# A transformer encoder in two fp32r halves: the weights' halves start at a different place in each chunk's buffers

## The chip, the cores and the metric

One core of a Trainium2 chip runs the kernel. The time is device microseconds from start to end of one execution; for a kernel on one core that is this core's time. Runs of a kernel are compared on the same chip. TensorE multiplies, VectorE and ScalarE do the element-wise work, GpSimd (POOL) helps, and SyncE (SP) issues the weights' loads.

## The reference

A two-layer encoder on one sequence of 256 tokens with 1024 channels, all in float32:

```
for l in range(2):
    h = rms_norm(x, g_mix[l])
    c_q, c_kv, k_r, qkv_b, qkv_c, gate_logits = split(h @ w_in[l])
    y_a = latent attention (8 heads)           # w_uq, w_ukv
    y_b = dilated banded attention (12 heads)
    y_c = neighbourhood attention with a bias (8 heads)
    gates = sigmoid(gate_logits)               # three of 1024
    merged = gates[0]*(y_a @ w_pa[l]) + gates[1]*(y_b @ w_pb[l]) + gates[2]*(y_c @ w_pc[l])
    x = x + merged @ w_o[l]
    h = rms_norm(x, g_ffn[l])
    x = x + (silu(h @ w1[l]) * (h @ w3[l])) @ w2[l]    # 2816 inner channels
return rms_norm(x, g_final)
```

## The kernel before

Every large product is made of fp32r pieces: an operand is cast to fp32r (its high half, hi), the rest is subtracted out (its low half, lo), and three products, hi x hi, hi x lo and lo x hi, are summed in PSUM. XH and XL are the halves of the normed input (8 blocks of 128 channels by 256 tokens), YH and YL those of the attention outputs, HL those of the merged and of the gated inner channels, chl those of the latent vectors.

The weights (158 MB with both layers) are packed on the host into 308 chunks, 154 for each layer, mostly 128 partitions by 1024 columns, in the order in which they are used (`plan`). Each chunk passes through three steps. `dma_next` loads it into one of 6 buffers `raw`, on SP's queue. `split_next` casts it to `hi` on ScalarE (line 292) and subtracts on VectorE to get `lo` (line 294), into one of 4 buffers each. `take` hands the pair to the products, and before that keeps the loads 6 chunks and the split 1 chunk ahead of the use.

`mm3` (line 320) makes the three products for one block of 128 x 128 weights and 256 tokens, all through line 318, where TensorE first loads the weights and then streams the other operand through. `n_tile` runs it for the 8 blocks of a chunk: 24 products into one half of a PSUM bank. The blocks of a chunk lie 512 bytes apart in each partition, the blocks of XH and XL 1024. In some parts the roles are exchanged: activations are loaded as weights, and hi or lo is streamed (values of the attentions, 256 or 288 columns; the last w2 products, 512 columns).

Each layer goes through projections and attentions (other small products between, from queues of units), the gate logits (24 chunks), the merge of the three branches with `w_o`, the first two inner blocks in 4 merged chunks `f`, and then 20 steps of w1, w3 and w2 chunks: the feed-forward. The order on each engine is that of a planner that simulates the program; a few instructions are tied to others by hand (`queue`).

Tiles are laid in SBUF one after another in a pool, each size rounded up to 32 bytes: first the pool `one` (X, XH, XL, C, G, YH, YL, RB, RT), then `ring` (raw, hi, lo), then `tmp` with everything else. `single` and the `tile_pool` lines show the sizes.

Of the kernel before, what the change touches and what calls it, by code (L numbers as in the profile page):

```python
# [11 lines left out]
F32R = mybir.dt.float32r  # L12
# [4 lines left out]
P = 128  # L17
# [210 lines left out]
def f32(ap):  # L228
    return ap.bitcast(F32)
# [3 lines left out]
def encoder(ctx: ExitStack, tc: tile.TileContext, x, w, gains, cst, rpb, gfin, out):  # L233
# [4 lines left out]
    ring = ctx.enter_context(tc.tile_pool(name="ring", bufs=4))  # L238
# [23 lines left out]
    def queue(ins, behind):  # L262
        info = mybir.DependencyInfo(mybir.DependencyClass.NoSync, mybir.DependencyReason.DATA)
        tc.add_manual_dep(ins, behind.name, info, reason="order")
# [21 lines left out]
    def split_next():  # L286
        i = at["split"]
        width = chunks[i][2]
        t = raw.pop(i)
        hi = ring.tile([P, 1024], F32R, tag="hi", name="hi", bufs=4)  # L290
        lo = ring.tile([P, 1024], F32R, tag="lo", name="lo", bufs=4)
        act.copy(hi[:, :width], t[:, :width])  # L292
        eng = pool if chunks[i][1] == ("f", 0) else dve
        ins = eng.tensor_sub(lo[:, :width], t[:, :width], f32(hi[:, :width])).ins  # L294
        if eng is dve and "hold" in at:
            queue(ins, at["hold"])
        split[i] = (hi, lo)
        at["split"] += 1

    def ahead(n_split, n_dma):  # L300
        n = len(chunks)
        while at["split"] < min(n, n_split):
            while at["dma"] <= at["split"]:
                dma_next()
            split_next()
        while at["dma"] < min(n, n_dma):
            dma_next()
# [813 lines left out]
```

## Time and profile before

| | |
|---|---|
| time, median of 3 runs | 926.07 us (923.6 to 926.31) |
| profiled execution: time, span | 925.92 us, 924.1 us |
| busy share of PE, PEld, DVE, ACT, POOL | 98%, 94%, 72%, 56%, 14% |
| granted TensorE clock, mean | 0.997 |
| bytes read from HBM | 157.64 MB, 172 GB/s over the span |

PE is TensorE's products, PEld its weight loads, which run beside products. A product's duration in the profile is from its start to the end of the last column's result, some 0.28 us, and products overlap; how fast they follow each other is seen from their start times in the timeline. A line of the chain of waits that says "5.60 PE ps_g L318 x48" means that for 5.60 us the end was set by 48 products in a row. Distances in bytes are counted in one partition, from the tile sizes in the code.

### The profile page before, as it was taken

Reading aid. Unit: us, or ns where it says so; the run is one execution under the profiler, and the core shown is the slowest. Engines: PE = TensorE matmul, PEld = TensorE weight load, DVE = VectorE, ACT = ScalarE, POOL = GpSimd, SP = SyncE. Lnnn points to the kernel's source line nnn. Section 1 sums busy time; section 2 is a strip of 40 time slices with the busy share of each in tenths; the row PEclk is TensorE's granted clock in tenths of the full one; section 3 lists DMA queues with packets and bytes.
Section 4 is the critical chain, followed back from the end, with each engine's and each line's share of the span. In section 5 each row is a group of like instructions: output and inputs, shape, how many; then the busy total and the mean of one; then the engine's idle time right before and its main releaser. Section 6 shows DMA issues by size and latency. Waiting matters only on the chain. (4 is left out here: it accounts for less than half of the span.)

```text
span 924.1 us, 18598 instructions
## 1 busy us (share of the span) xinstructions
PE 906.0 (98%) x7446; PEld 871.0 (94%) x7446; DVE 660.8 (72%) x1003; ACT 519.1 (56%) x858; POOL 128.9 (14%) x138
## 2 busy tenths in 40 slices
PE   8999999999999999999999999999999999999996
PEld 6999898999999999999999989899999999999995
DVE  6987877555888766666699888665577976666663
ACT  6776875533566544444477778655355654444443
POOL 2223112000022100000023240400000210000000
PEclk9999999999999999999999999999999999999998
DMA  8985455344675766655467644533457566555531
GB/s 290 286 289 174 133 149 150 107 153 148 193 223 183 258 209 195 184 185 184 119 237 213 211 147 135 173 117 124 145 178 214 168 212 205 184 193 184 195 124 45
DMA packets 53414, 166.71 MB, mean 180 GB/s; under 512 B 6736, under 2 KB 7504, under 8 KB 53328
## 3 DMA queue, kind: packets, MB, share of 16 engines
q1 hardware_dynamic: 48384, 158.69, 53.7%
q0 software_dynamic: 1920, 3.15, 1.6%
q10 hardware_dynamic: 3024, 3.69, 1.5%
q8 instruction: 58, 0.95, 0.4%
q14 instruction: 28, 0.23, 0.1%
HBM read 157.64 MB, written 1.05 MB: 172 GB/s over the span
## 5 line engine op out<-in xcount | busy, mean ns | idle before, releaser
L294 DVE TENSOR_TENSOR lo<-raw,hi 128x1024 fp32r<-128x1024 f32 (+4 forms) x306 | 373.3, 1227 | 153.4 <-ACT hi L292 152.1
L292 ACT CAST hi<-raw 128x1024 fp32r<-128x1024 f32 (+5 forms) x308 | 304.1, 992 | 301.8 <-PE ps_g L318 162.7
L318 PE MATMUL ps_g<-XH,hi 128*128 128x256 f32 x1392 | 390.0, 281 | 1.2 <-ACT hi L292 1.2
L318 PE MATMUL ps_g<-XH,lo 128*128 128x256 f32 x1392 | 387.9, 281 | 1.6 <-DVE lo L294 1.6
L318 PE MATMUL ps_g<-XL,hi 128*128 128x256 f32 x1392 | 389.3, 280 | 0.0
L318 PEld LDWEIGHTS ps_g<-XH,hi 128*128 128x128 f32 x1392 | 261.5, 188 | 5.2 <-issue 1.9
L318 PEld LDWEIGHTS ps_g<-XH,lo 128*128 128x128 f32 x1392 | 260.2, 188 | 5.3 <-issue 2.7
L318 PEld LDWEIGHTS ps_g<-XL,hi 128*128 128x128 f32 x1392 | 261.7, 188 | 1.6 <-issue 0.3
L318 PE MATMUL ps_acc<-HL,hi 128*128 128x256 f32 x608 | 109.3, 279 | 0.0
L318 PEld LDWEIGHTS ps_acc<-HL,hi 128*128 128x128 f32 x608 | 93.1, 188 | 0.0
L318 PE MATMUL ps_acc<-HL,lo 128*128 128x256 f32 x304 | 84.2, 280 | 0.0
L995 POOL TENSOR_TENSOR SG<-fab 128x256 f32<-128x256 f32 x44 | 34.5, 786 | 305.7 <-DVE fab L991 302.5
L318 PEld LDWEIGHTS ps_acc<-HL,lo 128*128 128x128 f32 x304 | 57.1, 188 | 0.0
L318 PE MATMUL ps_acc<-hi,HL 128*128 128x512 f32 x176 | 55.3, 395 | 0.0
L318 PE MATMUL ps_g<-hi,XL 128*128 128x256 f32 (+1 forms) x160 | 45.9, 287 | 0.0
L318 PE MATMUL ps_g<-hi,XH 128*128 128x256 f32 (+1 forms) x160 | 45.4, 284 | 0.0
L318 PE MATMUL ps_g<-lo,XH 128*128 128x256 f32 (+1 forms) x160 | 45.2, 285 | 0.0
L991 DVE TENSOR_TENSOR fab<-ps_g,RB 128x512 f32<-128x512 f32 x40 | 27.6, 691 | 21.9 <-PE ps_g L318 21.9
L528 ACT COPY pT<-ps_t 128x512 f32<-128x512 f32 (+1 forms) x48 | 26.0, 551 | 29.0 <-PE ps_t L518 21.8
L318 PEld LDWEIGHTS ps_acc<-hi,HL 128*128 128x128 f32 x176 | 31.7, 188 | 6.1
L318 PE MATMUL ps_acc<-lo,HL 128*128 128x512 f32 x88 | 34.8, 395 | 0.0
L834 POOL TENSOR_TENSOR t<-t,CSR 128x512 f32<-128x512 f32 x12 | 19.7, 1644 | 107.9 <-DMA t<-t 79.1
(194 smaller groups left out, 1263.0 us busy)
## 6 DMA issues: line engine op xcount, KB each, us to landing
raw<-in_w SPq DMA_DIRECT2D x250, 512.0 KB, 3.6
raw<-in_w SPq DMA_DIRECT2D x20, 384.0 KB, 3.1
raw<-in_w SPq DMA_DIRECT2D x16, 320.0 KB, 3.1
braw<-in_rpb SPq DMA_DIRECT2D x16, 256.0 KB, 5.2
raw<-in_w SPq DMA_DIRECT2D x16, 256.0 KB, 2.7
t<-t ACTq DMA_DIRECT2D x48, 64.0 KB, 4.4
raw<-in_w SPq DMA_DIRECT2D x4, 432.0 KB, 4.9
KCt<-KCt POOLq DMA_DIRECT2D x8, 128.0 KB, 5.8
```

Source lines behind the costliest of these rows:

```text
L292: act.copy(hi[:, :width], t[:, :width])
L294: ins = eng.tensor_sub(lo[:, :width], t[:, :width], f32(hi[:, :width])).ins
L318: pe.matmul(o, a, b, start=start, stop=stop, skip_group_check=True)
L528: act.copy(u.pT[:, :n], u.tr[:, :n])
L834: pool.tensor_mul(t13, t13, bc(SR, 2))
L991: dve.tensor_mul(ab, o.rearrange("p (n s) -> p n s", n=2), bc(RB, 2))
L995: pool.tensor_mul(s[:, 1, :], ab[:, 0, :], ab[:, 1, :])
```

## The change

In the n-th chunk (n counts over both layers) hi and lo no longer begin at the start of their buffers, but 4 (n mod 14) columns, 16 (n mod 14) bytes, after it. The buffers get 52 columns more, which is the largest such shift. What is loaded, cast, subtracted and multiplied is the same, in the same order; the tiles that are laid after these buffers move up by the added bytes.

```diff
--- before.py
+++ after.py
@@ -287,8 +287,10 @@
         i = at["split"]
         width = chunks[i][2]
         t = raw.pop(i)
-        hi = ring.tile([P, 1024], F32R, tag="hi", name="hi", bufs=4)
-        lo = ring.tile([P, 1024], F32R, tag="lo", name="lo", bufs=4)
+
+        skew = slice(4 * (i % 14), 4 * (i % 14) + 1024)
+        hi = ring.tile([P, 1024 + 52], F32R, tag="hi", name="hi", bufs=4)[:, skew]
+        lo = ring.tile([P, 1024 + 52], F32R, tag="lo", name="lo", bufs=4)[:, skew]
         act.copy(hi[:, :width], t[:, :width])
         eng = pool if chunks[i][1] == ("f", 0) else dve
         ins = eng.tensor_sub(lo[:, :width], t[:, :width], f32(hi[:, :width])).ins
```

## Rows read from the trace of the kernel before

**Rows 1.** Page, part 1: busy us (share of the span) and instructions of each engine.
```profile
PE 906.0 (98%) x7446; PEld 871.0 (94%) x7446; DVE 660.8 (72%) x1003; ACT 519.1 (56%) x858; POOL 128.9 (14%) x138
```

**Rows 2.** Waits of TensorE: line, releaser, us in total, times, longest us.
```profile
PE ps_s L318 <- POOL KB L836: 2.6, 2, 1.5
...
PE ps_g L318 <- DVE lo L294: 1.6, 3, 0.6
...
PE ps_g L318 <- ACT hi L292: 1.2, 1, 1.2
```

**Rows 3.** Chain of waits in order of time: start us, us, products.
```profile
706.28 2.83 PE ps_acc L318 x24
...
764.57 5.60 PE ps_g L318 x48
770.17 2.79 PE ps_acc L318 x12
```

**Rows 4.** Windows: us, each engine's busy us and operations, granted clock, DMA.
```profile
186.00:226.00 40.00, 40.00 (x341) 40.00 (x341) 20.76 (x24) 13.49 (x15) 0.00 (x0) 1.00 0.47 145
...
304.00:454.00 150.00, 150.00 (x1284) 150.00 (x1283) 97.85 (x109) 68.00 (x91) 14.16 (x18) 1.00 0.63 196
...
760.00:900.00 140.00, 140.00 (x1001) 130.98 (x1000) 91.69 (x102) 63.09 (x84) 12.60 (x17) 1.00 0.56 181
```

**Rows 5.** Timeline: transposes in the feed-forward of layer 1.
```profile
743.02 1.47 PE L1003 MATMUL ps_acc<-C,X 128*128 128x128 f32 x12
```

**Rows 6.** Groups: line, engine, tiles, shapes, count, busy us, mean ns, idle before.
```profile
L294 DVE TENSOR_TENSOR lo<-raw,hi 128x1024 fp32r<-128x1024 f32 (+4 forms) x306 | 373.3, 1227 | 153.4 <-ACT hi L292 152.1
L292 ACT CAST hi<-raw 128x1024 fp32r<-128x1024 f32 (+5 forms) x308 | 304.1, 992 | 301.8 <-PE ps_g L318 162.7
L318 PE MATMUL ps_g<-XH,hi 128*128 128x256 f32 x1392 | 390.0, 281 | 1.2 <-ACT hi L292 1.2
...
L318 PE MATMUL ps_acc<-HL,hi 128*128 128x256 f32 x608 | 109.3, 279 | 0.0
...
L318 PE MATMUL ps_acc<-hi,HL 128*128 128x512 f32 x176 | 55.3, 395 | 0.0
L318 PE MATMUL ps_g<-hi,XL 128*128 128x256 f32 (+1 forms) x160 | 45.9, 287 | 0.0
...
L318 PE MATMUL ps_g<-YL,hi 128*128 128x256 f32 x96 | 27.0, 281 | 0.0
...
L318 PE MATMUL ps_c<-YH,hi 128*128 128x256 f32 x64 | 18.0, 282 | 0.0
```

**Rows 7.** Timeline: ends of the first w1 tile, layer 0, then layer 1.
```profile
287.66 0.28 PE L318 MATMUL ps_g<-XH,hi 128*128 128x256 f32 x1
...
290.37 0.28 PE L318 MATMUL ps_g<-XH,lo 128*128 128x256 f32 x1
...
740.73 0.28 PE L318 MATMUL ps_g<-XH,lo 128*128 128x256 f32 x1
...
742.48 0.28 PE L318 MATMUL ps_g<-XH,lo 128*128 128x256 f32 x1
```

**Rows 8.** Timeline: the first merged chunk f, layer 0.
```profile
276.19 0.28 PE L318 MATMUL ps_f<-XH,hi 128*128 128x256 f32 x1
...
279.07 0.28 PE L318 MATMUL ps_f<-XH,hi 128*128 128x256 f32 x1
```

**Rows 9.** Timeline: products of the latent tile, layer 0.
```profile
46.78 0.39 PE L318 MATMUL ps_a<-chl,hi 128*128 128x256 f32 x2
...
47.46 0.39 PE L318 MATMUL ps_a<-chl,hi 128*128 128x256 f32 x2
```

**Rows 10.** Timeline: products of the attention outputs in the merge.
```profile
225.53 0.28 PE L318 MATMUL ps_g<-YH,hi 128*128 128x256 f32 x1
...
228.37 0.28 PE L318 MATMUL ps_g<-YH,hi 128*128 128x256 f32 x1
```

## Prediction

> **What bounds the kernel now.** I read the page's first part first: TensorE's products are busy for 906.0 of 924.1 us and its weight loads for 871.0, while VectorE stands at 72% [rows 1]. The table of waits, cut to TensorE, comes next: six groups of waits, 9.5 us in all, the longest 2.6 us [rows 2]. So no load, cast or subtraction is late. The end is set by how fast TensorE starts one product after another, and the change can move it in only two ways: by that rhythm, or by making the two halves late.
>
> The page's list of costly groups shows 281 ns for a product, but that is a latency; neighbours overlap. The rhythm is read from start times. In the first tile of the feed-forward 23 steps take from 287.66 to 290.37, 117.8 ns each [rows 7]; later in that stretch the chain has pieces of 48 products in 5.60 us, 116.7 ns each [rows 3]. Over long windows: 40 us hold 341 products and 150 us hold 1,284. As the products in flight at both edges are counted, I add one latency of 0.28 us and get 118.1 and 117.0 ns. [...] A stream of transposes, which move 128 columns instead of 256 behind weights of the same size, starts every 109 ns (12 in 1.47 us, less one latency, over 11) [rows 5]. So about 8 ns of each product is something other than its weight load, and this is what the change could reach.
>
> **Part 1: the rhythm.** Products that read hi or lo, counted from the groups (the third product of a trio has half the count where two share hi): 3 x 1392 and 3 x 160 into ps_g, 608 + 304 into ps_acc, 3 x 96 into ps_g and 3 x 64 into ps_c from YH and YL, as many as the latter into ps_f, together 6,240 of about 256 columns, and 176 + 88 = 264 of 512 columns [rows 6]. So 1 ns of rhythm is worth 6.2 us.
>
> Where operands lie follows from the tile sizes, each rounded up to 32 bytes: hi and lo start 224 bytes (modulo 512) past XH and XL, 448 past HL and the latent tile chl, 32 past YH. All slices step by multiples of 512, so these distances now hold for every product of a kind. After the change a buffer has 4,304 bytes, laid out as 4,320. So the four buffers of a ring fall 224 bytes further each, lo lies 17,280 instead of 16,384 past hi, and the skew adds 16 times (n mod 14). Every chunk gets other distances, and the odd chunks start at 16 modulo 32, where now every operand starts on a multiple of 32.
>
> Does the rhythm depend on the distance? One and the same tile (first w1 tile of the feed-forward, distance 224) runs at the 117.8 ns named above in layer 0 and at 116.7 ns in layer 1 (15 steps in 1.75 us) [rows 7]. The first merged chunk f, at distance 224 too, holds exactly 120.0 ns (24 steps in 2.88 us) [rows 8]. At distance 448, chl runs at 113.3 ns (6 steps in 0.68 us) [rows 9], and HL at 117.9 (24 in 2.83) [rows 3]. At distance 32, YH runs at 118.3 ns (24 steps in 2.84 us) [rows 10]. So one distance allows several steady rhythms, and which one a stretch falls into is set by how it was entered. They lie between 113.3 and 120.0 at every distance the trace has.
>
> What I expect is that the new starts make TensorE enter a rhythm anew at nearly every chunk, and that the rhythms are drawn from the same set. Mean now: 1,920 products of the feed-forward (40 tiles of 24, two layers) at 116.7, 2,016 of logits and merge at 118.1, the other 2,304 at about 117.0 as in the long window, gives 117.3 ns. Mean of the five rhythms 113.3, 116.7, 117.8, 118.3 and 120.0: 117.2 ns; without the lowest, which is seen only over short stretches, 118.2. I count the lowest as rarely met and take 117.4, nearer to the first: +0.1 ns x 6,240 = +0.6 us. The 264 wide products (2.79 us for 12, 232 ns each [rows 3]) I leave as they are; 4 ns either way is 1 us. Bounds of this part, from rows: all at the transposes' 109 ns, -8.3 x 6,240 = -52 us; all at 120.0, +2.7 x 6,240 = +17 us.
>
> [...]
>
> **Part 2: the halves.** The cast (ScalarE, 308 times, 992 ns) and the subtraction (VectorE, 306 times, 1,227 ns) now write to other starts, and the subtraction reads one [rows 6]. No row shows such a start. Nothing below zero is likely to matter: both engines wait for TensorE already. Above: in the feed-forward window VectorE is busy 91.7 of 140 us and ScalarE 63.1 [rows 4]; if every subtraction took half as long again, 102 operations of which three in six are subtractions of 1.23 us add at most 31 us, still 123 of 140. So the cover holds and I take 0. If it were gone (twice as long), VectorE would need some 154 of 140 us there, and the whole kernel would lose at least 28 us over both layers.
>
> **Part 3: the rest.** No instruction, DMA or wait is added; the DMA writes go to raw, which does not move. SP's and the other queues keep their order. The 1,792 bytes more push the tiles allocated later by the same amount: they keep their distances among themselves, and their distances to X and the halves are part of what is redrawn above. 0 us.
>
> **Sum.** The profiled run took 925.92 us (924.1 span and 1.8 around it), 0.15 below the median 926.07. 926.07 + 0.6 = 926.7 us.
>
> **Rivals.**
> The start of a chunk has no say at all. The rhythm would then come from the order of work alone, as one tile with two rhythms suggests [rows 7]. Time 926.1. Against it: HL, YH and XH do keep different rhythms through long stretches. [...]
>
> Faster: the distances that are odd multiples of 16 bytes, which the trace never has, keep weight load and product out of each other's way, and the odd chunks, half of the products, fall to 113.3 ns as chl does [rows 9]: -4.0 x 3,120 = -12.5 us, 913.6 us. For it: this rhythm exists and 109 is possible [rows 5]. Against it: five kinds of product at three distances all lose about 8 ns.
>
> Slower, one mechanism in the odd chunks: a load or stream that starts at 16 modulo 32 touches one unit more. The rhythms differ by steps of some 3.3 ns (113.3, 116.7, 120.0), and I price it as one such step on each product of an odd chunk: 3.3 x (3,120 + 132) = +10.7 us, 936.8 us. It decides as soon as the added step isn't hidden in the 8 ns that a load has to spare (116.7 less 109).
>
> Slower, the good rhythm is lost: the feed-forward's 116.7 is held only because distances are the same chunk after chunk. All fall to YH's 118.3: +1.0 x 6,240 = +6.2 us, 932.3 us.
>
> **How the numbers follow.** Chances: forecast 0.31 (own range 922 to 932), no say 0.12, faster by odd distances 0.24, one step more 0.18, good rhythm lost 0.15. A measurement of this kernel can tell about 0.3% (2.8 us) from no change. Faster: 0.04 of the forecast and 0.23 of the third, 0.27. Slower: 0.07, 0.17 and 0.12, 0.36. Within 0.3%: 0.37. The range reaches to both outer cases, 912 to 938; beyond it lie all products at 109 or at 120, and late halves, under 2 in 10.
>
> **What would show it.** Starts inside a chunk's 24 products: if the forecast is right, the chunks in the feed-forward no longer all take 2.80 us, some 2.72 and some 2.88, with mean near 2.82. If the start has no say, all still take 2.80. If parity decides, odd and even chunks differ. If the halves are late, TensorE's waits for hi and lo grow from 2.8 us [rows 2]. I am wrong if the mean rhythm leaves 116.9 to 118.0 ns, or if waits grow by over 3 us.

## The result, and the profile after

The changed kernel takes 930.58 us (median of 4) against 924.88 us of the kernel before on the same chip: ratio 1.0066, 95% interval 1.0044 to 1.0087. That is slower by 0.66%, inside the range that I gave and on the side to which I gave 0.36, but beyond the 0.3% within which I had put my forecast of 926.7 us.

The page of the changed kernel, part 1, in the columns of [rows 1]:

```profile
PE 912.2 (98%) x7446; PEld 877.9 (95%) x7446; DVE 665.5 (72%) x1003; ACT 518.5 (56%) x858; POOL 129.2 (14%) x138
```

TensorE is busy 6.2 us longer with the same number of products, and the span grew by 4.4 us (924.1 to 928.5). Its waits, the answer to [rows 2], all six groups:

```profile
PE ps_s L320 <- POOL KB L838: 1.9, 2, 1.1
PE ps_f L320 <- DVE XL L397: 1.7, 2, 0.9
PE ps_g L320 <- ACT hi L294: 1.3, 1, 1.3
PE warm L320 <- DVE warm L615: 1.2, 1, 1.2
PE ps_t L520 <- DVE p L515: 0.9, 2, 0.6
PE ps_g L320 <- DVE lo L296: 0.5, 1, 0.5
```

They sum to 7.5 us, 2 less than before. So nothing came late; the time is in the rhythm. A small part of the 6.2 us lies elsewhere: in the first 25 us the granted clock was 0.93 in this execution and 1.00 in that of the kernel before, and TensorE was busy for 21.95 us there against 20.98. The windows of [rows 4] show the rest:

```profile
186.00:226.00 40.00, 40.00 (x341) 39.93 (x339) 20.50 (x24) 13.78 (x15) 0.00 (x0) 1.00 0.48 145
304.00:454.00 150.00, 150.00 (x1271) 150.00 (x1270) 96.66 (x109) 66.44 (x90) 13.44 (x17) 1.00 0.63 195
760.00:900.00 140.00, 140.00 (x998) 131.31 (x997) 90.58 (x100) 62.85 (x83) 11.88 (x16) 1.00 0.56 185
```

In layer 0's feed-forward 1,271 products fit where 1,284 did, 118.2 instead of 117.0 ns (150.28 us over the count). In the first window, in the logits, the count of 341 is the same as before, but one product more or less is 0.35 ns there; by the start times the steps in it grew from 117.8 to 118.6 ns. The granted clock is 1.00 in both. The chain in the feed-forward of layer 1, the answer to [rows 3], no longer repeats:

```profile
793.53 5.69 PE ps_g L320 x48
799.22 2.78 PE ps_acc L320 x12
802.00 5.59 PE ps_g L320 x48
807.59 2.80 PE ps_acc L320 x12
810.39 5.70 PE ps_g L320 x48
816.09 2.79 PE ps_acc L320 x12
818.88 5.54 PE ps_g L320 x48
```

Where every 48 products took 5.60 us, they now take 5.54 to 5.71. One level deeper, two neighbouring chunks of layer 1 in the timeline, each by the first and last line of a stretch:

```profile
743.26 0.28 PE L320 MATMUL ps_g<-XH,hi 128*128 128x256 f32 x1
...
745.64 0.28 PE L320 MATMUL ps_g<-XH,hi 128*128 128x256 f32 x1
...
748.44 0.28 PE L320 MATMUL ps_g<-XH,hi 128*128 128x256 f32 x1
...
750.24 0.29 PE L320 MATMUL ps_g<-XH,hi 128*128 128x256 f32 x1
```

The first (n = 246) makes 21 steps in 2.38 us, 113.3 ns; it is the tile that ran at 116.7 ns before [rows 7]. The second (n = 247) makes 15 steps in 1.80 us, 120.0 ns. Counted from the tile sizes, the weights of n = 246 start 64 bytes (modulo 128) past XH, those of n = 247 48 bytes, if the first, fourth, second and third buffer of a ring take the chunks with n modulo 4 = 0, 1, 2 and 3. This order stands in no trace. Of the 24 possible ones it is among the four that separate the distances most, and the one of these by which 64 is the low distance; so the table below counts only together with the runs of one constant distance, which need no such order. These figures made me sort all products of tiles with XH and XL by the distance of the next weights' start from the start of the stream beside which they load, modulo 128, and take the mean step from their start times (over 400 steps for each figure, steps at waits left out):

| distance | 0 | 16 | 32 | 48 | 64 | 80 | 96 | 112 |
|---|---|---|---|---|---|---|---|---|
| before, ns | | | | | | | 116.9 | |
| changed, ns | 118.7 | 118.3 | 118.9 | 118.9 | 115.2 | 118.3 | 118.5 | 117.6 |

Over all kinds of product the same count gives +4.7 us, of which +4.6 are XH's and XL's tiles; the span's difference is 4.4. Within a tile the weights of a product and those of the next one start alike modulo 128, so no run here tells which of the two counts against the stream.

### The profile page after: what moved, and what is told of

It is laid out like the page before. It is cut to its first block, busy times and chain, and to the rows that moved or that the text cites. A ratio compares the mean times of both kernels' runs of the same rounds, so it can differ in the third digit from the quotient of the medians.

```text
span 928.5 us, 18598 instructions
## 1 busy us (share of the span) xinstructions
PE 912.2 (98%) x7446; PEld 877.9 (95%) x7446; DVE 665.5 (72%) x1003; ACT 518.5 (56%) x858; POOL 129.2 (14%) x138
## 5 line engine op out<-in xcount | busy, mean ns | idle before, releaser
L296 DVE TENSOR_TENSOR lo<-raw,hi 128x1024 fp32r<-128x1024 f32 (+4 forms) x306 | 374.7, 1232 | 156.1 <-ACT hi L294 154.7
L515 DVE TENSOR_SCALAR p<-p,m 128x256 f32<-128x256 f32 (+1 forms) x80 | 33.4, 453 | 1.4
```

Source lines behind the costliest of these rows:

```text
L515: dve.tensor_scalar_mul(u.p[:, ps], u.p[:, ps], u.m[:, 2 + hh : 3 + hh])
```

## The experiments

Four theories. A: the rhythm depends on that distance modulo 128, and the change trades one fairly good distance (96) for a mix of all. B: any start that changes from chunk to chunk breaks a steady rhythm. C: starts at 16 modulo 32 cost a step each. D: it is the wider buffers and the tiles moved by them, not the skew. Each experiment is an edit of the kernel before. Times are medians against the kernel before on the same chip.

**The wider buffers alone** (wide_no_skew), here as the edit of the changed kernel:

```diff
-        skew = slice(4 * (i % 14), 4 * (i % 14) + 1024)
+        s = 0
+        skew = slice(s, s + 1024)
```

> Buffers 52 columns longer, every chunk at their start (the skew alone is undone). Theory A, distance: the rhythm follows the start of the weights less the start of the stream beside which they load, modulo 128 bytes; the four buffers then stand at 96, 64, 32 and 0, with 118.5, 115.2, 118.9 and 118.7 ns in the changed kernel's trace, mean 117.8 against 117.0 before, +0.8 x 4,200 = +3.5 us, 928.4 us. Theory B, change: any change of distance from chunk to chunk breaks the steady rhythm, about 930.5. Theory C, starts at 16 modulo 32 cost a step: none left, 925. Theory D, the wider buffers and the moved tiles cost it all: 930.6.

Measured: 930.95 against 925.16 us, ratio 1.0070 (1.0051 to 1.0088): all of the loss, without any skew. The longer buffers already spread the four of a ring over four distances. By distance, in the same order of buffers: 118.5 ns at 0, 119.8 at 32, 115.8 at 64, 118.7 at 96. (The profiled execution took 934.25 us; its granted clock was 0.93 in the first 25 us and 0.96 from 140 to 180.) D would be enough here; A is right in its pattern and low in its sum by 2.5 us, in part because 32 came at 119.8. C is out as the only cause.

**The skew alone** (skew_mod8), in buffers whose length is a multiple of 128 bytes:

```diff
+        s = 4 * (i % 8)
+        skew = slice(s, s + 1024)
+        hi = ring.tile([P, 1024 + 32], F32R, tag="hi", name="hi", bufs=4)[:, skew]
```

(and so for lo.) 

> Skew of 16 (n mod 8) bytes in buffers only 32 columns longer, so that the four buffers of a ring stand alike modulo 128 (the skew alone is done). A: all eight distances in equal shares, mean 118.1 ns, +1.1 x 4,200 = +4.6 us, 929.5 us, and the chunks at distance 64 near 114. B: 930. C: half of the chunks slow, 930. D: 925.

Measured: 930.5 us, ratio 1.0057 (1.0042 to 1.0072). Again nearly all of the loss, so D isn't needed, and the two parts don't add: each alone mixes the distances, and both together only mix them. One expectation missed: the chunks at 64 ran at 117.5 ns, not near 114, and those at 96 were the lowest, at 117.1; the six others lay between 118.4 and 119.7. So 64 doesn't always bring its low rhythm.

**One distance for all chunks.** The next four hold the skew constant, so that no start changes from chunk to chunk, in buffers of 1024 + 32 columns:

```diff
+        s = 24
+        skew = slice(s, s + 1024)
```

(24 columns for const96, 8 for const32, 4 for const16, 12 for const48.)

> Every chunk begins 96 bytes into its buffer, so weights stand 64 (modulo 128) past XH and XL in every chunk. A: 114.0 to 115.2 ns, -2 to -3 ns x 4,200 = -8 to -12 us, some +0.7 us from HL whose distance becomes 32: 913 to 918 us. B, C and D: nothing changes from chunk to chunk, no odd start: 925 us.

Measured: 920.63 us, ratio 0.9947 (0.9931 to 0.9964), faster than the kernel before. XH's and XL's tiles run at 115.2 ns, the upper end of what A gave; YH, now at distance 0, lost 0.8 ns, and HL, at 32, 1.1 ns. The range of my sum ended 2.6 us too low, and these two explain only a part of that.

> Every chunk begins 32 bytes into its buffer: distance 0 modulo 128 to XH and XL in every chunk. A: 118.7 ns as in the changed kernel, +1.7 x 4,200 = +7 us, 932 us. B, C and D: 925 us.

Measured: 932.48 us, ratio 1.0076 (1.0061 to 1.0091). XH's and XL's tiles at 119.2 ns; YH, which this shift puts at 64, went from 118.3 to 114.9 ns. Const96 and const32 differ by 64 bytes and stand on both sides of the kernel before. That is A, and neither B nor C: nothing changes from chunk to chunk and no start is odd.

> Every chunk begins 16 bytes into its buffer: all starts at 16 modulo 32, distance 112 to XH and XL. A: 117.6 to 119.6 ns there (the two traces with all eight distances), +0.6 to +2.6 x 4,200, 927.5 to 936, and 116.9 to 118.7 for YH and HL, 0 to +0.5 us. C, a step of 3.3 ns for each product with a start at 16 modulo 32: +21 us, 946. B: 925.

Measured: 933.11 us, ratio 1.0079 (1.0058 to 1.0100), 119.1 ns at distance 112. All starts at 16 modulo 32 cost no more than const32, whose starts all are multiples of 32: C's extra step isn't there.

> Every chunk begins 48 bytes into its buffer: distance 16 modulo 128. A: 118.3 ns as in the two traces with all eight distances, +1.3 x 4,200 = +5.5 us, 931 us. B: 925.

Measured: 932.84 us, ratio 1.0083 (1.0068 to 1.0098), 118.7 ns at distance 16.

The stretch 304 to 454 us of three of them, first const96, in the columns of [rows 4]:

```profile
304.00:454.00 150.00, 150.00 (x1291) 150.00 (x1290) 97.76 (x108) 68.92 (x91) 14.15 (x18) 1.00 0.63 196
```

then const32:

```profile
304.00:454.00 150.00, 150.00 (x1264) 150.00 (x1263) 95.99 (x107) 65.78 (x88) 13.42 (x17) 1.00 0.62 195
```

and const16:

```profile
304.00:454.00 150.00, 150.00 (x1266) 150.00 (x1265) 96.62 (x109) 66.52 (x89) 13.39 (x17) 1.00 0.62 195
```

1,291, 1,264 and 1,266 products in the same 150 us, 1,284 before: 64 bytes of shift move the rhythm by 2.5 ns (116.4 to 118.9).

**Starts that change, at one distance** (alt128): `s = 32 * (i % 2)` columns, that is 0 or 128 bytes, so the distance to XH and XL stays 96 modulo 128.

> The kernel before with buffers 32 columns longer, odd chunks beginning 128 bytes into theirs: starts change from chunk to chunk, the distance to XH and XL stays 96 modulo 128 as before. Theory A, distance modulo 128: the rhythms of before, 116.7 to 117.8 ns, 924 to 927 us. Theory B, each change of a start costs: as the changed kernel, 930 us.

Measured: 924.59 against 925.70 us, ratio 0.9994 (0.9982 to 1.0006): no change in time. B's 930 is out. But two shifts stand behind the equal time. In the profiled run, the fastest of the eleven, XH's and XL's products took 117.4 instead of 117.0 ns, some 1.5 us over 4,368 of them, a third of what the change cost them; and HL's 912 took 114.3 instead of 117.8 ns at their unchanged distance of 64, 3.2 us the other way (more on that below). So at distance 96 a start that differs from chunk to chunk costs little, and 96 and 224 bytes do nearly alike; that it costs nothing isn't shown.

**All operands at distance 64** (pads64_32): no skew, but unused bytes between the tiles,

```diff
+    single("PAD0", [P, 16])
     YH = single("YH", [P, 10, S], F32R)
     YL = single("YL", [P, 10, S], F32R)
     RB = single("RB", [P, S])
     RT = single("RT", [P, 2])
+    single("PAD1", [P, 8])
```

> The kernel before with 64 unused bytes ahead of YH and 32 ahead of the ring, no skew: weights stand 64 (modulo 128) past XH, XL, YH, YL, HL and chl alike. Theory A, distance: XH and XL products 115.2 ns as with the constant 96, -1.8 x 4,200 = -7.6 us, YH and YL 115, -1.6 us, the exchanged products 116.5, -0.6 us: 915 us; if no stretch is entered in the wrong rhythm any more, 113.3 ns for nearly all, 907 us. Theory B, change: nothing changes from chunk to chunk, 925 us.

Measured: 917.03 against 925.53 us, ratio 0.9903 (0.9882 to 0.9925): 1% faster than the kernel before with 96 bytes of padding, and 2 us above the first of A's two figures. The same stretch holds 1,306 products:

```profile
304.00:454.00 150.00, 150.00 (x1306) 150.00 (x1306) 98.14 (x109) 68.83 (x91) 14.19 (x18) 1.00 0.63 198
```

This run also answers a rival that I had not written down: that only the weights' own start counts, not its distance from the stream. In const96 and here hi and lo lie 96 bytes (modulo 128) further than before, but YH's products took 119.1 ns there, at distance 0, and 113.5 here, at 64. So the distance counts.

Its chain in the feed-forward of layer 1 shows that distance 64 has two rhythms:

```profile
755.11 5.66 PE ps_g L320 x48
760.77 2.80 PE ps_acc L320 x12
763.57 5.46 PE ps_g L320 x48
769.03 2.79 PE ps_acc L320 x12
771.82 5.66 PE ps_g L320 x48
777.48 2.80 PE ps_acc L320 x12
780.27 5.46 PE ps_g L320 x48
```

5.46 us for 48 is 113.8 ns, 5.66 is 117.9, in strict alternation though all starts of weights and streams repeat alike modulo 128. The two PSUM banks of ps_g alternate in the same way; but they do so in layer 0 too, and there, from its fourth step on, every w1 and w3 tile runs at 113.3 to 113.7, while w2 tiles, on HL, run at 117.8. From the timeline there, XH's tile first and HL's behind it:

```profile
318.92 0.28 PE L320 MATMUL ps_g<-XH,hi 128*128 128x256 f32 x1
...
321.30 0.28 PE L320 MATMUL ps_g<-XH,hi 128*128 128x256 f32 x1
...
321.64 0.40 PE L320 MATMUL ps_acc<-HL,hi 128*128 128x256 f32 x2
...
324.12 0.40 PE L320 MATMUL ps_acc<-HL,hi 128*128 128x256 f32 x2
```

21 steps in 2.38 us, 113.3 ns, and 21 in 2.48, 118.1.

**The same with starts that change, and its control.** pads_alt128 adds the alternation by 128 bytes to it, in buffers 32 columns longer; pads_wide has only the longer buffers. The two differ in `s` alone.

> The same with buffers 32 columns longer, odd chunks beginning 128 bytes into theirs: the start changes from chunk to chunk, the distance modulo 128 doesn't. A: as pads64_32 within 2 us. B: each change costs, +5 us over pads64_32. If the distance counts modulo 256 instead, half of the chunks are at another one, about +8 us over pads64_32.

> pads64_32 with buffers 32 columns longer and no shift in them (between pads64_32 at 917.0 and pads_alt128 at 921.0). A, with two rhythms at distance 64 (113.3 and 117.8) of which a stretch takes one by how it was entered: anything from 915 to 922, each chunk of the feed-forward at one of the two. B: the alternation made the 4 us, so 917.

Measured: pads_alt128 920.96 us (0.9945, 0.9925 to 0.9964), pads_wide 916.55 against 925.70 us (0.9900, 0.9884 to 0.9915). A's 2 us for pads_alt128 was missed by 2. The longer buffers, whose four starts lie 128 bytes further each, cost nothing beside pads64_32 (0.9900 and 0.9903), so as far as the time goes 128 bytes are a period here. The alternation in them cost 4.4 us (0.9945 against 0.9900, intervals apart), as B had it for this pair, though the distance modulo 128 stayed; A's 915 to 922 for pads_wide holds 916.55 too, but doesn't give the difference. The stretch 304 to 454 us, first pads_wide:

```profile
304.00:454.00 150.00, 150.00 (x1296) 150.00 (x1295) 97.79 (x108) 68.45 (x91) 14.16 (x18) 1.00 0.63 196
```

then pads_alt128:

```profile
304.00:454.00 150.00, 150.00 (x1276) 150.00 (x1275) 97.07 (x107) 68.79 (x91) 14.12 (x18) 1.00 0.62 194
```

The chunks of pads_alt128 run at the two rhythms too, but 117.8 far more often: nearly all of layer 0's feed-forward, odd and even chunks alike. So, as these runs read, the distance modulo 128 has a say in which rhythms a stretch can have, and something more, which a change of starts can disturb, in which of them it takes. Whether the changing start does that by itself, or by the way in which this program then enters its stretches, these runs don't tell.

## Why the prediction came out as it did

**What bounds the kernel** was right: TensorE's rhythm. Waits stayed small (9.5 to 7.5 us), VectorE's load of the feed-forward window fell in with the smaller number of products (91.7 to 90.6 of 140 us), and the subtraction took 1,232 ns where it took 1,227. Parts 2 and 3, both taken at 0, hold.

The time lies in my range, but the range was wide enough for every rival; the centre, +0.6 us, was wrong, against +5.7 measured.

**The step that failed is the mean of the five rhythms.** I read from one tile with two rhythms [rows 7] that every distance draws from one set, though my rows had 113.3 at distance 448 alone, and counted the lowest, 113.3 ns, part of the way into the mean: 117.4 ns, +0.6 us. The runs show otherwise. Nine w1 and w3 tiles of the changed kernel's feed-forward hold 113.4 ns over 13 or more steps in a row; by the order of buffers above, eight of them stand at one distance of eight, 64, and one at 32. What the mix of the eight gives is 118.1 to 118.4. The mean without the lowest, 118.2 ns, stood in the same paragraph; it would have given +0.9 x 6,240 = +5.6 us and 931.7 us, against 930.6 measured. Two of the rows that I used had already stood at that distance: chl at 113.3 and HL at 117.9 are both at 448, which is 64 modulo 128 [rows 3, 9]. They are its two rhythms.

**Which products lose.** I gave every kind of product the same term. In fact HL, YH and the exchanged products stood near the mean of all distances before and stayed there (HL 117.8 before, 118.3 after), and the loss is that of XH's and XL's tiles, 4.6 us over 4,368 products, mainly in the feed-forward, which had held 116.7.

**The rivals.** "The good rhythm is lost" (932.3 us, chance 0.15) is what happened: the feed-forward's 116.7 was lost and became 118.2. But that the distance was the same in each chunk isn't what had held it: held at 0 (const32) the rhythm is 119.2, held at 64 (const96) 115.2; it was the distance 96 that was kept. "The start has no say" is refuted by const96 and const32: a shift by 96 bytes in every chunk gave 920.63 us, one by 32 bytes 932.48. "Odd distances are free" is refuted by const16 and const48 (933.11 and 932.84 us); the good distance is even, 64. "One step more at 16 modulo 32" is refuted by const16 beside const32 (933.11 and 932.48 us).

**The marks** that I set: chunks of the feed-forward would spread from 2.72 to 2.88 us with mean near 2.82. They do spread just so (113.3 to 120.1 ns times 24), and their mean is 2.83 (5.66 us for 48). I was to be wrong if the mean rhythm left 116.9 to 118.0 ns; by the steps it is 118.1, just outside.

## What to carry to other kernels

When TensorE is full of short fp32r products, each with its own weights, read the steps between start times, not the durations (here some 117 ns against 0.28 us), and sort them by where the two operands start against each other: here the best distance was 64 bytes modulo 128 (115.2 ns in const96, against 119.2 at 0 in const32), and 96 bytes of padding were worth 1%. The skew that spread the starts was no cure; it bought the average of all distances, good ones and bad ones, 118.1 ns for 116.9. First find the good distance, then hold it everywhere, for tiles between the buffers too, whose lengths move it (52 columns more in each buffer cost 0.70% in wide_no_skew), and leave the starts as steady as they were: at distance 64 an alternation by 128 bytes took back some 4 of 9 us.

## What the runs showed of the hardware that I had not expected

At distance 64 products ran for tens of microseconds near either of two rhythms, 113.3 and 117.8 ns: 344 products of layer 1's logits took 39.20 us in pads64_32 (114.0 ns each), and 1,276 took the 150 us of pads_alt128 (117.8). The rhythm changed at a chunk's boundary (pads64_32, at 321.64 us, 113.3 to 118.1 ns) or a few products behind it (the changed kernel, in the tile that starts at 328.7 us: steps of 117, 120 and 119 ns, then 20 at 113.4). What selects between them stays open, and so does why 64 modulo 128 is the good one. Distances 32, 48 and 80 were not run as constants for XH and XL; YH and HL stood there in const96, const16 and const48, at 117.7 to 118.9 ns. If every product of XH and XL in pads64_32 held 113.3 instead of 114.6 ns on average, it would be worth another 1.3 x 4,200 = 5 us.

Within a steady chunk the steps repeat within 1 ns (in a w3 tile of layer 1 before: 120, 113, 116 and 118 or 117 ns, over and over). Whether ScalarE's and VectorE's work beside TensorE has a say in the rhythm, no run tested.
